# One weight pool for all stages, gate banks copied out beside the statistics, and pooled inputs ahead of their gates

## Chip, cores and metric

The kernel runs on one core of one Trainium2 chip. The metric is the device time of one execution in microseconds (us), as the median of several runs; lower is better. One further execution was recorded by the hardware profiler, and all rows below are of that one. Engines are named as the profile names them: PE is TensorE (PEld its weight loads), DVE VectorE, ACT ScalarE, POOL GpSimd, SP SyncE, which here issues every DMA.

## What is computed

One inference step of a single layer for 1024 prompt tokens and 8 x 4 decode tokens, 1056 rows in all, in float32:

```python
h = rmsnorm(x, norm_w)
pool_in, pool_z, qk_pre, v, o_pre, m_z, if_pre, gate_pre = jnp.split(h @ w_in, SPLIT_OFFSETS, axis=-1)
a, pool_hist_new = multiscale_pool(pool_in, pool_hist, pos0, pool_w, pool_scale)
a = (a * jax.nn.silu(pool_z)) @ w_pool_down
qk, conv_hist_new = causal_conv_silu(qk_pre, conv_hist, conv_w, conv_b)
...                                       # mLSTM over chunks of 128 tokens: gate statistics, then attention
bm = (hc * jax.nn.silu(m_z)) @ w_mlstm_down
g_a, g_b = jnp.split(jax.nn.sigmoid(gate_pre), 2, axis=-1)
x = x + (g_a * a + g_b * bm) @ w_out
x = x + (pe @ w_ple) * jax.nn.sigmoid(rmsnorm(x, ple_norm_w) @ w_ple_gate)
```

`multiscale_pool` takes causal means over windows of 2, 4, 8 and 16 tokens, one window for each of four groups of 256 channels, subtracts the input, and multiplies each group by a 256 x 256 matrix `pool_w`. The decode tokens also update a 512 x 512 state C for each of 8 sequences and 4 heads (32 states of 1 MB, each read and written once).

## The kernel before

Every large product is split: a weight tile of 4 x 128 rows and 256 columns comes by one 512 KB DMA into a buffer with the tag `wraw`, ACT rounds it to `whi` (line 370) and DVE forms the rest, `wlo` (line 376); PE then runs three matmuls for each product of hi and lo parts (`mm3`, lines 383 to 385). `load_w` (from line 396) does this for a block of 256 output columns, two such tiles for a depth of 1024; `fm` then runs two halves (f = 0, 1) of 128 output features, each over 1056 tokens in 3 pieces of 352 columns (72 matmuls) or 4 pieces of 264 (96 matmuls). Each piece fills a PSUM bank of the tag `mm`, of which there are two, and an eviction (`ev`) empties it; so PE may run one piece ahead of the evictions.

The stages that matter here, in the order of the program:

1. The first projections (lines 163 and 221), 28 blocks of seven steps, in pools `weights1` (seven `wraw`, three `whi`, three `wlo`) and `gemm`. Beside the last three steps `gate_rows` (line 757) projects the eight input and forget gates and stores them (lines 764, 766).
2. `weights1` is closed, `const2` and `weights2` (two `wraw`, three `whi`, three `wlo`) are opened where it lay, and `masks` (lines 504 to 527) forms a few constants on POOL and DVE.
3. `merge_gates` over six groups of 256 gate columns. Each half is evicted by three sigmoids on ACT (line 1311) into a tile `sz` of 1056 columns, of which there are two, and stored to `sgD` (line 1313). After each `fm` the function `tick` moves a background generator on. At first that is `gates`: the gates' statistics, a chain of small instructions on DVE, ACT, PE and SP, with Exp and Ln on ACT, and its end, 12 loads of `dt` (line 882), DVE sums on them (886, 888), four exponentials of 1536 columns (line 905) and their stores (907). Then the generator is the prompt's attention, and after it `sample`, the decode states.
4. `pool_branch`, for each of four groups: pool_z by `load_w` and `fm` with Silu into two `sz` (line 1219), pool_in by `load_w` and `fm` with the windowed sums on DVE (1260 to 1275) and the split into `poh` and `pol`, and the pooled product with `pool_w`, 36 matmuls on `poh` and `pol`, whose eviction (line 1286) multiplies `sz`; `sz` is then stored to `actD` (1289). Beside this run the 32 decode states: a load of `ct` (line 1166), PE lines 1168 and 1172, DVE line 1173, a store (1176).
5. The last two gate groups, the down projections and the tail, which the change does not touch.

The engine queues are filled in an order that a list scheduler fixes when the kernel is built: it takes, for each engine, the ready instruction that comes first in the program by its own model of time. Each engine then runs its queue strictly in that order, so an instruction that waits holds all behind it. SP's queue of DMA issues is such a queue too.

Of the kernel before, what the change touches and what calls it, by code (L numbers as in the profile page):

```python
# [12 lines left out]
AF = mybir.ActivationFunctionType  # L13
# [5 lines left out]
P = 128  # L19
# [101 lines left out]
class FeatBlock(Block):  # L121
# [10 lines left out]
    def prep(self, i):  # L132
# [11 lines left out]
        elif i in "db":  # L144
            x = tr.t(tr.wp, [P, 4, 256], "wraw", bufs=tr.nraw)
            tt(out=x[:, :, f1], in0=r1[:, :, f2], in1=r2[:, :, f2], op=ALU.add)
            tt(out=x[:, :, f2], in0=r1[:, :, f1], in1=x[:, :, f1], op=ALU.subtract)
            hi, lo = tr.split_w(x)
            self.w["d"], self.w["b"] = [(hi[:, :, f], lo[:, :, f]) for f in (f1, f2)]
            self.x = x  # L150
        elif i in ("c", "01"):
            tt(out=r1[:, :, f2], in0=r1[:, :, f1], in1=r1[:, :, f2], op=ALU.subtract)
            tt(out=r1[:, :, f1], in0=r2[:, :, f1], in1=self.x[:, :, f2], op=ALU.add)
            hi, lo = tr.split_w(r1)
            self.w["01"], self.w["c"] = [(hi[:, :, f], lo[:, :, f]) for f in (f1, f2)]
# [28 lines left out]
class TokBlock(Block):  # L184
# [15 lines left out]
    def prep(self, i):  # L200
        tr, r = self.tr, self.raw
        tt = tr.nc.vector.tensor_tensor
        if i == "d":
            self.x = tr.t(tr.wp, [P, 4, 256], "wraw", bufs=tr.nraw)
            tt(out=self.x, in0=r[0][1], in1=r[1][1], op=ALU.add)
# [135 lines left out]
class Trunk:  # L341
    def __init__(self, ctx, nc, tc, I, O):
        self.ctx, self.nc, self.tc, self.I, self.O = ctx, nc, tc, I, O
        self.n = 0
        self.bg = None
        self.held = None


# [6 lines left out]
    def t(self, pool, shape, tag, dt=F32, bufs=1):  # L355
        self.n += 1
        return pool.tile(list(shape), dt, name=f"{tag}_{self.n}", tag=tag, bufs=bufs)

    def mmps(self):
# [36 lines left out]
    def load_w(self, ap, n, scale=None):  # L396
# [4 lines left out]
        for k0 in range(0, kt, 4):  # L401
            kk = min(4, kt - k0)
            raw = self.t(self.wp, [P, 4, 256], "wraw", bufs=self.nraw)
            nc.sync.dma_start(raw[:, :kk, :n], ap[k0 * P:(k0 + kk) * P].rearrange("(k p) n -> p k n", p=P))
# [99 lines left out]
    def masks(self):  # L504
        nc, c = self.nc, self.cp2
        one = self.t(self.mk, [P, P], "one")
        nc.gpsimd.memset(one, 1.0)
        tri = self.t(self.mk, [P, P], "tri")
        nc.gpsimd.affine_select(out=tri, in_=one, pattern=[[1, P]], compare_op=ALU.is_ge, fill=0.0, base=0,
# [13 lines left out]

        cnt = self.t(self.mk, [P, 16], "cnt")
        nc.gpsimd.iota(cnt, pattern=[[1, 16]], base=1, channel_multiplier=0, allow_small_or_imprecise_dtypes=True)
# [3 lines left out]
    def norm_in(self, blocks):  # L529
# [103 lines left out]

        ab = self.t(self.wp, [P, 4, 256], "wraw", bufs=self.nraw).rearrange("p (i a) n -> p i (a n)", i=2)
        a = [ab[:, 0], ab[:, 1], st(), st()]
# [56 lines left out]
    def raw_w(self, w, c0, f, ks=(0, 1)):  # L692

        out = []
        for k in ks:
            r = self.t(self.wp, [P, 4, 256], "wraw", bufs=self.nraw)
            c = c0 + 256 * f
# [70 lines left out]
    def gates(self):  # L768
# [67 lines left out]
        mc = mcs[:, 0:1]  # L836
        yield True
        nc.vector.scalar_tensor_tensor(out=m[:, :L], in0=b[:, :L], scalar=mc, in1=m[:, :L], op0=ALU.add, op1=ALU.max)
        bm = self.t(a, [R, W], "gbm")
# [359 lines left out]
    def pool_branch(self):  # L1199
# [8 lines left out]
        for g in range(4):  # L1208
            win = 2 ** (g + 1)
            h1 = self.t(a, [DB * PH, 256], "ph1")  # L1210
            nc.sync.dma_start(h1, hist[:, g * 256:(g + 1) * 256])
            w = self.load_w(I["w_in"][:, O_PZ + g * 256:O_PZ + (g + 1) * 256], 256)
            sz = []
            for f in range(2):
                z = self.t(a, [P, NT], "sz", bufs=2)

                def ev(j, ps, z=z):
                    s = slice(j * CW, (j + 1) * CW)
                    nc.scalar.activation(z[:, s], ps[:, :CW], AF.Silu)
                self.fm(w, f, self.hmov, ev)  # L1220
                sz.append(z)
            w = self.load_w(I["w_in"][:, O_PIN + g * 256:O_PIN + (g + 1) * 256], 256)
            pooled = []
            for f in range(2):
# [6 lines left out]
                def ev(j, ps, f=f, ft=ft, ph=ph, pl=pl, prev=prev):  # L1231
# [46 lines left out]
                    self.lo(pl[:, c], po, ph[:, c])  # L1278
                self.fm(w, f, self.hmov, ev, CH)
            w = self.load_w(I["pool_w"][g], 256)  # L1280
            for f in range(2):
# [19 lines left out]
    def merge_gates(self, groups):  # L1301
        nc, I = self.nc, self.I
        for gg in groups:
            x, g = gg // 4, gg % 4
            w = self.load_w(I["w_in"][:, O_GA + gg * 256:O_GA + (gg + 1) * 256], 256)
            for f in range(2):
                z = self.t(self.pp, [P, NT], "sz", bufs=2)

                def ev(j, ps, z=z):
                    s = slice(j * CW, (j + 1) * CW)  # L1310
                    nc.scalar.activation(z[:, s], ps[:, :CW], AF.Sigmoid)  # L1311
                self.fm(w, f, self.hmov, ev)
                nc.sync.dma_start(self.sgD[x][g * 2 + f], z)

# [233 lines left out]
    def run(self):  # L1548
# [26 lines left out]
        self.xp, _x = self.pool("sums", "right")  # L1575
        self.wp, _w = self.pool("weights1")
        self.gp, _g = self.pool("gemm")
        self.nraw, self.nsb, self.nz = 7, 6, 7
        blocks = []
# [14 lines left out]
        _g.close()  # L1594
        _w.close()
        _x.close()
# [3 lines left out]
        self.hcS = self.t(self.cp2, [P, H, 4, NS], "hcS")  # L1600
        self.wp, _w = self.pool("weights2")
        self.nraw = 2
        self.mk, _m = self.pool("mask", "right")
        self.masks()
        _m.close()
        self.ap_, _a = self.pool("gates", "right")
# [4 lines left out]
        def rest():  # L1611
            self.rate = 1.6
            yield from gates
            _a.close()
            self.atp, _at = self.pool("attn", "right")
# [36 lines left out]
        self.tail_ple()  # L1652
        for st in (_l, _f, _w, _c2, _c, _ps):
            st.close()
# [24 lines left out]
```

## Time and profile before

| | |
|---|---|
| median of 3 runs | 2232.88 us (2228.46 to 2236.81) |
| the profiled execution | 2232.33 us |
| its span, first to last instruction | 2230.6 us |
| PE busy | 2159.6 us |
| DVE busy | 1257.2 us |
| ACT busy | 900.8 us |
| mean granted TensorE clock, as a share of full speed | 0.990 |

The span is the time that the instructions of the profile cover; 1.7 us of the execution lie outside it. Busy time of PE is modelled for pipelined matmuls, so a busy PE is not one at its peak, and a gap of PE is a lower bound of what was lost there: after a long gap the rows show matmuls at half the clock.

### The profile page before, as it was taken

The page shows a single profiled execution, that of the slowest core. Times are in us where ns is not written, and L with a number is a line of the kernel's source. Part 1 is how long each engine was busy: PE and PEld are TensorE (multiplying, and loading weights), DVE is VectorE, ACT ScalarE, POOL GpSimd, SP SyncE. Part 2 cuts the span into 40 slices and gives each one's busy share as a digit, 9 for nine tenths or more (in the row PEclk, how much of TensorE's full clock was granted, in tenths as well). Part 3 has the DMA queues.
Part 4 walks back from the last instruction along what each step waited for, and adds up shares of the span by engine and source line. Part 5 has one row for each costly group of instructions (what it writes and reads, how often), then busy time and mean ns, then how long its engine had stood idle before and what let it go on. Part 6 is the DMA issues. An engine that isn't in the chain of part 4 may idle for free.

```text
span 2230.6 us, 40176 instructions
## 1 busy us (share of the span) xinstructions
PE 2159.6 (97%) x16407; PEld 2054.8 (92%) x16407; DVE 1257.2 (56%) x2172; ACT 900.8 (40%) x1791; POOL 122.7 (6%) x335
## 2 busy tenths in 40 slices
PE   7999999999999999899999899999988999999998
PEld 6899999999999999899999798787778999999998
DVE  6855576456746565446566675576563243543645
ACT  5645455444635353633333343222223331213443
POOL 1100001000101000000000100000000000000000
PEclk9999999999999999999999999999999999999999
DMA  4233333333233331675655645887774343323112
GB/s 153 85 107 108 102 103 96 108 102 115 93 107 96 112 93 38 195 245 160 196 158 161 204 140 175 294 289 261 252 265 162 97 139 102 108 97 104 53 48 83
DMA packets 238601, 312.72 MB, mean 140 GB/s; under 512 B 13994, under 2 KB 170066, under 8 KB 238416
## 3 DMA queue, kind: packets, MB, share of 16 engines
q1 hardware_dynamic: 238416, 310.15, 42.8%
q8 instruction: 129, 2.11, 0.4%
q14 instruction: 56, 0.46, 0.1%
HBM read 200.01 MB, written 110.45 MB: 139 GB/s over the span
## 4 chain that ended last, share of the span: by engine, by line
PE 87%; DMA 6%; DVE 3%; ACT 2%; SPq 1%; issue 1%; POOL 0%; DVEq 0%; POOLq 0%; ACTq 0%
PE mm L221 21%; PE mm L163 14%; PE mm L383 12%; PE mm L385 12%; PE mm L384 12%; PE num L1168 2%; PE misc L953 2%; PE num L383 1%; PE kv L383 1%; PE num L384 1%; PE num L385 1%; PE kv L384 1%; PE kv L385 1%; PE kv L1172 1%; DMA o<-oD 1%; DMA ct<-state_mlstm_C 1%
## 5 line engine op out<-in xcount | busy, mean ns | idle before, releaser
L376 DVE TENSOR_TENSOR wlo<-wraw,whi 128x1024 fp32r<-128x1024 f32 (+1 forms) x220 | 238.7, 1086 | 228.7 <-ACT whi L370 222.9
L370 ACT ACTIVATE whi<-wraw 128x1024 fp32r<-128x1024 f32 (+1 forms) x220 | 209.2, 951 | 340.8 <-PE mm L221 107.1
L383 PE MATMUL mm<-hh,whi 128*128 128x352 f32 (+1 forms) x832 | 265.7, 319 | 14.5 <-ACT sz L1311 9.0
L385 PE MATMUL mm<-hh,wlo 128*128 128x352 f32 (+1 forms) x832 | 262.6, 316 | 0.0
L384 PE MATMUL mm<-hl,whi 128*128 128x352 f32 (+1 forms) x832 | 261.7, 315 | 0.0
L221 PE MATMUL mm<-wlo,hh 128*128 128x256 f32 x768 | 216.1, 281 | 0.0
L221 PE MATMUL mm<-whi,hl 128*128 128x256 f32 x768 | 215.9, 281 | 0.0
L221 PE MATMUL mm<-whi,hh 128*128 128x256 f32 x768 | 214.6, 279 | 0.0
L383 PEld LDWEIGHTS mm<-hh,whi 128*128 128x128 f32 x832 | 158.8, 191 | 28.5 <-ACT sz L1311 11.3
L384 PEld LDWEIGHTS mm<-hl,whi 128*128 128x128 f32 x832 | 159.2, 191 | 5.7 <-issue 4.4
L385 PEld LDWEIGHTS mm<-hh,wlo 128*128 128x128 f32 x832 | 158.7, 191 | 5.5 <-issue 4.2
L323 DVE SCALAR_TENSOR_TENSOR z<-z,vcols,z 128x556 f32<-128x556 f32 x192 | 146.8, 794 | 8.4 <-ACT z L321 6.6
L163 PE MATMUL mm<-hh,whi 128*128 128x264 f32 x512 | 148.4, 290 | 1.0 <-DVE z L179 0.6
L163 PE MATMUL mm<-hl,whi 128*128 128x264 f32 x512 | 146.2, 286 | 0.4 <-DVE hl L376 0.3
L163 PE MATMUL mm<-hh,wlo 128*128 128x264 f32 x512 | 145.5, 284 | 0.0
L221 PEld LDWEIGHTS mm<-whi,hh 128*128 128x128 f32 x768 | 144.7, 188 | 0.0
L221 PEld LDWEIGHTS mm<-whi,hl 128*128 128x128 f32 x768 | 144.6, 188 | 0.0
L221 PEld LDWEIGHTS mm<-wlo,hh 128*128 128x128 f32 x768 | 144.3, 188 | 0.2
L1173 DVE SCALAR_TENSOR_TENSOR ct<-ct,dec,kv 128x512 f32<-128x512 f32 x128 | 93.4, 744 | 70.9 <-PE kv L1172 61.3
L385 PE MATMUL mm<-mvhB,wlo 128*128 128x352 f32 x384 | 123.2, 322 | 0.0
L384 PE MATMUL mm<-mvlB,whi 128*128 128x352 f32 x384 | 123.0, 322 | 0.0
L383 PE MATMUL mm<-mvhB,whi 128*128 128x352 f32 x384 | 122.1, 324 | 0.0
(462 smaller groups left out, 6071.6 us busy)
## 6 DMA issues: line engine op xcount, KB each, us to landing
wraw<-w_in SPq DMA_DIRECT2D x112, 512.0 KB
ct<-state_mlstm_C SPq DMA_DIRECT2D x32, 1024.0 KB
new_C_sample<-ct SPq DMA_DIRECT2D x32, 1024.0 KB
qkD<-z SPq DMA_DIRECT2D x64, 256.0 KB
qk<-qkD SPq DMA_DIRECT2D x16, 1024.0 KB
sgD<-sz SPq DMA_DIRECT2D x16, 528.0 KB
sg<-sgD SPq DMA_DIRECT2D x16, 528.0 KB
vD<-z SPq DMA_DIRECT2D x32, 256.0 KB
```

The lines of the kernel that those rows point to most:

```text
L163: self.tr.nc.tensor.matmul(ps[:, j, :CH], lhsT=st[:, k], rhs=mv[k][:, c], start=start and k == 0 and n == 0, stop=stop and k == 3 and n == ...
L221: self.tr.nc.tensor.matmul(ps[:, t // 2, t % 2 * 256:t % 2 * 256 + 256], lhsT=st[k][:, c], rhs=mv[:, k], start=start and t % 2 == 0 and k ...
L323: nc.vector.scalar_tensor_tensor(out=acc, in0=z[:, o:o + tot], scalar=wc(o), in1=acc, op0=ALU.mult, op1=ALU.add)
L370: self.nc.scalar.activation(out, in_, AF.Copy)
L376: self.nc.vector.tensor_tensor(out=out, in0=in_, in1=hi.bitcast(F32), op=ALU.subtract)
L383: mm(ps, lhsT=sh, rhs=mh, start=start, stop=False)
L384: mm(ps, lhsT=sh, rhs=ml, start=False, stop=False)
L385: mm(ps, lhsT=sl, rhs=mh, start=False, stop=stop)
L953: nc.tensor.matmul(out, lhsT=qk[:, 4 + d, i * L:(i + 1) * L], rhs=qk[:, d, i * L:], start=d == 0, stop=d == 3)
L1168: nc.tensor.matmul(num[32 * d:32 * d + 32, 0, :], lhsT=qm[:, b * P + d * NS:b * P + (d + 1) * NS], rhs=ct[:, d, :], start=b == 0, stop=b = ...
L1172: nc.tensor.matmul(kv, lhsT=km[:, d * P:(d + 1) * P], rhs=vst, start=True, stop=True)
L1173: nc.vector.scalar_tensor_tensor(out=ct[:, d, :], in0=ct[:, d, :], scalar=self.dec[:, h * DB + b, 1:2], in1=kv, op0=ALU.mult, op1=ALU.add)
```

## The change

Three things are changed. (1) `weights1` and `weights2` become one pool `weights` that stays open to the end (two `wraw`, three `whi`, three `wlo`), and a pool `weights1` with five more raw buffers (`wrawx`) that closes after the first projections. `raw()` hands out the seven in turn, and the two alone afterwards. `masks` moves into the generator `gates`, behind its first pause, and takes its scratch tiles from the pool of that generator. (2) While the generator is inside `gates`, `merge_gates` evicts a bank by a plain copy on DVE, and one sigmoid on ACT over the whole tile of 1056 columns follows. The flag is read before each `fm`. (3) In `pool_branch` the block that forms pool_z moves from ahead of pool_in to behind it.

```diff
+    def raw(self):
+        self.nraw += 1
+        if self.wx is not None and self.nraw % 7 > 1:
+            return self.t(self.wx, [P, 4, 256], "wrawx", bufs=5)
+        return self.t(self.wp, [P, 4, 256], "wraw", bufs=2)
...
@@ load_w, raw_w, Block.prep, norm_in
-            raw = self.t(self.wp, [P, 4, 256], "wraw", bufs=self.nraw)
+            raw = self.raw()
...
@@ gates
         mc = mcs[:, 0:1]
         yield True
+        self.masks()
...
@@ pool_branch
-            w = self.load_w(I["w_in"][:, O_PZ + g * 256:O_PZ + (g + 1) * 256], 256)
-            sz = []
-            for f in range(2):
-                ...
             w = self.load_w(I["w_in"][:, O_PIN + g * 256:O_PIN + (g + 1) * 256], 256)
             pooled = []
             ...
                 self.fm(w, f, self.hmov, ev, CH)
+            w = self.load_w(I["w_in"][:, O_PZ + g * 256:O_PZ + (g + 1) * 256], 256)
+            sz = []
+            for f in range(2):
+                z = self.t(a, [P, NT], "sz", bufs=2)
+                ...
+                self.fm(w, f, self.hmov, ev)
+                sz.append(z)
             w = self.load_w(I["pool_w"][g], 256)
...
@@ merge_gates
-                def ev(j, ps, z=z):
+                plain = self.stats
+                def ev(j, ps, z=z, plain=plain):
                     s = slice(j * CW, (j + 1) * CW)
-                    nc.scalar.activation(z[:, s], ps[:, :CW], AF.Sigmoid)
+                    if plain:
+                        nc.vector.tensor_copy(z[:, s], ps[:, :CW])
+                    else:
+                        nc.scalar.activation(z[:, s], ps[:, :CW], AF.Sigmoid)
                 self.fm(w, f, self.hmov, ev)
+                if plain:
+                    nc.scalar.activation(z, z, AF.Sigmoid)
                 nc.sync.dma_start(self.sgD[x][g * 2 + f], z)
...
@@ run
-        self.wp, _w = self.pool("weights1")
+        self.wp, _w = self.pool("weights")
+        self.wx, _wx = self.pool("weights1")
...
-        _w.close()
+        _wx.close()
+        self.wx = None
...
-        self.wp, _w = self.pool("weights2")
-        self.nraw = 2
-        self.mk, _m = self.pool("mask", "right")
-        self.masks()
-        _m.close()
...
+            self.stats = True
             yield from gates
+            self.stats = False
```

## Rows read from the trace of the kernel before

**Rows 1.** The page: busy time, share of the span and instructions of each engine.

```profile
PE 2159.6 (97%) x16407; PEld 2054.8 (92%) x16407; DVE 1257.2 (56%) x2172; ACT 900.8 (40%) x1791; POOL 122.7 (6%) x335
```

**Rows 2.** Busy time by stretch (start:end, length, then each engine), granted clock, DMA.

```profile
895.00:899.40 4.40, 0.00 (x1) 0.01 (x1) 0.03 (x1) 2.12 (x3) 3.19 (x6) 0.82 0.99 315
899.40:909.60 10.20, 10.20 (x48) 9.88 (x48) 5.99 (x13) 7.06 (x8) 0.00 (x0) 0.74 0.42 123
909.60:933.90 24.30, 24.30 (x159) 23.67 (x158) 7.62 (x32) 10.69 (x18) 0.00 (x0) 1.00 0.51 140
933.90:950.20 16.30, 12.59 (x74) 11.44 (x72) 9.50 (x37) 16.09 (x17) 0.00 (x0) 1.00 0.96 300
...
1190.00:1345.00 155.00, 142.44 (x1062) 134.92 (x1061) 109.75 (x224) 63.26 (x131) 13.00 (x19) 0.97 0.53 167
```

**Rows 3.** What PE waited for from 895 to 1000: total us, times, longest.

```profile
PE mm L383 <- ACT whi L370: 4.5, 1, 4.5
PE mm L383 <- ACT sz L1311: 3.7, 4, 2.2
```

**Rows 4.** SP's queue in order of time: start, us, line, DMA, count.

```profile
893.41 1.02 SPq L404 DMA_DIRECT2D wraw<-w_in  x2
...
921.41 13.21 SPq L882 DMA_DIRECT2D dt<-bmD  x12
...
936.52 0.45 SPq L1313 DMA_DIRECT2D sgD<-sz  x1
...
945.49 0.33 SPq L1313 DMA_DIRECT2D sgD<-sz  x1
```

**Rows 5.** ACT in order of time, while PE waits for its evictions.

```profile
934.54 1.28 ACT L1311 ACT_TABLE_LOAD   x1
935.83 0.46 ACT L1311 ACTIVATE sz<-mm 128x352 f32<-128x352 f32 x1
936.32 1.28 ACT L905 ACT_TABLE_LOAD   x1
937.61 1.49 ACT L905 ACTIVATE dt<-dt 128x1536 f32<-128x1536 f32 x1
...
958.30 0.47 ACT L1311 ACTIVATE sz<-mm 128x352 f32<-128x352 f32 x1 [2.67 <-issue]
```

**Rows 6.** Groups of instructions by line and shape, 895 to 1400: busy us, mean ns.

```profile
L370 ACT ACTIVATE whi<-wraw 128x1024 fp32r<-128x1024 f32 x16 | 17.0, 1060 | 16.5 <-PE mm L384 13.2 <-DMA wraw<-w_in 3.2
L1025 DVE COPY C<-kv 128x256 f32<-128x256 f32 x16 | 6.7, 418 | 1.1 <-PE kv L385 1.1
L872 DVE COPY tok<-misc 128x128 f32<-128x128 f32 x1 | 0.3, 292 | 0.1
```

**Rows 7.** DVE in order of time: the first instructions of the masks.

```profile
890.08 0.79 DVE L517 TENSOR_REDUCE bcol<-ident 32x8 f32<-32x32 f32 x4
```

**Rows 8.** Stretches of the four pooled products, and the gate columns after the last.

```profile
1402.50:1416.00 13.50, 11.76 (x70) 8.12 (x69) 11.95 (x22) 3.51 (x9) 0.34 (x2) 1.00 1.03 367
1480.30:1492.50 12.20, 10.92 (x64) 8.21 (x61) 11.34 (x23) 2.90 (x8) 1.41 (x2) 1.00 0.77 261
1555.20:1568.00 12.80, 10.99 (x64) 8.25 (x61) 12.46 (x26) 2.69 (x7) 0.67 (x3) 1.00 0.81 277
1632.20:1654.10 21.90, 16.27 (x78) 9.92 (x75) 17.88 (x37) 5.28 (x12) 0.59 (x3) 0.84 0.77 257
1654.10:1688.50 34.40, 34.40 (x207) 31.68 (x206) 11.26 (x16) 10.49 (x18) 0.55 (x1) 1.00 0.77 265
```

**Rows 9.** PE in order of time: last pool_in matmul of the fourth group.

```profile
1630.97 0.28 PE L385 MATMUL mm<-hh,wlo 128*128 128x264 f32 x1
```

**Rows 10.** DVE in order of time: weights' and pooled input's low parts, fourth group.

```profile
1630.96 1.22 DVE L376 TENSOR_TENSOR wlo<-wraw,whi 128x1024 fp32r<-128x1024 f32 x1
1632.10 0.49 DVE L1260 TENSOR_TENSOR win<-win 128x324 f32<-128x324 f32 x1
1632.51 1.22 DVE L376 TENSOR_TENSOR wlo<-wraw,whi 128x1024 fp32r<-128x1024 f32 x1
...
1649.34 0.42 DVE L376 TENSOR_TENSOR pol<-po,poh 128x264 fp32r<-128x264 f32 x1
```

**Rows 11.** ACT in order of time: the split that feeds the first of those.

```profile
1629.48 1.06 ACT L370 ACTIVATE whi<-wraw 128x1024 fp32r<-128x1024 f32 x1 [0.45 <-PE mm L384]
```

**Rows 12.** What PE waited for from 1340 to 1760: total us, times, longest.

```profile
PE mm L383 <- ACT sz L1311: 6.9, 2, 5.3
PE num L1168 <- DMA ct<-state_mlstm_C: 6.0, 4, 3.7
```

More of the change, by code (lines that the diff above doesn't have):

```diff
@@ L144, in prep @@
         elif i in "db":
-            x = tr.t(tr.wp, [P, 4, 256], "wraw", bufs=tr.nraw)
+            x = tr.raw()
             tt(out=x[:, :, f1], in0=r1[:, :, f2], in1=r2[:, :, f2], op=ALU.add)
@@ L203, in prep @@
         if i == "d":
-            self.x = tr.t(tr.wp, [P, 4, 256], "wraw", bufs=tr.nraw)
+            self.x = tr.raw()
             tt(out=self.x, in0=r[0][1], in1=r[1][1], op=ALU.add)
@@ L505, in masks @@
         nc, c = self.nc, self.cp2
-        one = self.t(self.mk, [P, P], "one")
+        one = self.t(self.ap_, [P, P], "one")
         nc.gpsimd.memset(one, 1.0)
-        tri = self.t(self.mk, [P, P], "tri")
+        tri = self.t(self.ap_, [P, P], "tri")
         nc.gpsimd.affine_select(out=tri, in_=one, pattern=[[1, P]], compare_op=ALU.is_ge, fill=0.0, base=0,
@@ L522, in masks @@
         nc.vector.tensor_scalar(out=self.smask, in0=self.smask, scalar1=-1.0, scalar2=-NEG, op0=ALU.add, op1=ALU.mult)
-        cnt = self.t(self.mk, [P, 16], "cnt")
+        cnt = self.t(self.ap_, [P, 16], "cnt")
         nc.gpsimd.iota(cnt, pattern=[[1, 16]], base=1, channel_multiplier=0, allow_small_or_imprecise_dtypes=True)
@@ L632, in norm_in @@
         st = lambda: self.t(g, [P, HH], "s", bufs=self.nsb)[:, :HT]
-        ab = self.t(self.wp, [P, 4, 256], "wraw", bufs=self.nraw).rearrange("p (i a) n -> p i (a n)", i=2)
+        ab = self.raw().rearrange("p (i a) n -> p i (a n)", i=2)
         a = [ab[:, 0], ab[:, 1], st(), st()]
@@ L695, in raw_w @@
         for k in ks:
-            r = self.t(self.wp, [P, 4, 256], "wraw", bufs=self.nraw)
+            r = self.raw()
             c = c0 + 256 * f
@@ L1211, in pool_branch @@
             nc.sync.dma_start(h1, hist[:, g * 256:(g + 1) * 256])
-            w = self.load_w(I["w_in"][:, O_PZ + g * 256:O_PZ + (g + 1) * 256], 256)
-            sz = []
-            for f in range(2):
-                z = self.t(a, [P, NT], "sz", bufs=2)
-                def ev(j, ps, z=z):
[L1218 to L1221, printed above, removed]
             w = self.load_w(I["w_in"][:, O_PIN + g * 256:O_PIN + (g + 1) * 256], 256)
@@ L1279, in pool_branch, with ev @@
                 self.fm(w, f, self.hmov, ev, CH)
+            w = self.load_w(I["w_in"][:, O_PZ + g * 256:O_PZ + (g + 1) * 256], 256)
+            sz = []
+            for f in range(2):
+                z = self.t(a, [P, NT], "sz", bufs=2)
+                def ev(j, ps, z=z):
+                    s = slice(j * CW, (j + 1) * CW)
+                    nc.scalar.activation(z[:, s], ps[:, :CW], AF.Silu)
+                self.fm(w, f, self.hmov, ev)
+                sz.append(z)
             w = self.load_w(I["pool_w"][g], 256)
@@ L1307, in merge_gates @@
                 z = self.t(self.pp, [P, NT], "sz", bufs=2)
-                def ev(j, ps, z=z):
+                plain = self.stats
+                def ev(j, ps, z=z, plain=plain):
                     s = slice(j * CW, (j + 1) * CW)
-                    nc.scalar.activation(z[:, s], ps[:, :CW], AF.Sigmoid)
+                    if plain:
+                        nc.vector.tensor_copy(z[:, s], ps[:, :CW])
+                    else:
+                        nc.scalar.activation(z[:, s], ps[:, :CW], AF.Sigmoid)
                 self.fm(w, f, self.hmov, ev)
+                if plain:
+                    nc.scalar.activation(z, z, AF.Sigmoid)
                 nc.sync.dma_start(self.sgD[x][g * 2 + f], z)
@@ L1575, in run @@
         self.xp, _x = self.pool("sums", "right")
-        self.wp, _w = self.pool("weights1")
+        self.wp, _w = self.pool("weights")
+        self.wx, _wx = self.pool("weights1")
         self.gp, _g = self.pool("gemm")
-        self.nraw, self.nsb, self.nz = 7, 6, 7
+        self.nraw, self.nsb, self.nz = -1, 6, 7
         blocks = []
@@ L1612, in rest @@
             self.rate = 1.6
+            self.stats = True
             yield from gates
+            self.stats = False
             _a.close()
@@ L1652, in run @@
         self.tail_ple()
-        for st in (_l, _f, _w, _c2, _c, _ps):
+        for st in (_l, _f, _c2, _w, _c, _ps):
             st.close()
```

## Prediction

> **What bounds the kernel now.** I read the busy times first: PE is busy for 2159.6 us of a span of 2230.6, its weight loads lie beside that, and no other engine is busy for more than 57% [rows 1]. The change takes no matmul away, so all it can move is the 71 us in which PE stands still and what its clock loses after such gaps. Next I read PE's waits and the table of stretches where the change acts. At the seam between the first projections and the gate columns PE has a gap of 4.4 us [rows 2], nearly all of it one wait of 4.5 for a weight's high part [rows 3]. The 48 matmuls behind it take 10.2 us at a mean granted clock of 0.74, while 159 of the next stretch take 24.3 at full clock (some of those are tiny), 0.153 each [rows 2]. At that rate the 48 would take 7.3, so the slow clock costs another 2.9. From 933.9 to 950.2 PE is busy 12.6 of 16.3 us: 3.7 go in four waits for the sigmoid that empties a bank [rows 2, 3]. In the pool stage PE rarely shows as idle, so I compared matmuls per microsecond. In the four stretches of the pooled product it does 70, 64, 64 and 78 in 60.4 us; the gate columns after them run 207 in 34.4, 6.0 per us, at which the 276 would take 46.0 [rows 8]. That is 14.4 us lost, about half of it in the fourth group. Together the addressable loss is 4.5 + 2.9 + 3.7 + 14.4 = 25.5 us, 1.1%.
>
> **Part 1, one weight pool.** The two loads for the first gate columns are issued at 893.41 [rows 4], when the last projection step is nearly over. In the changed kernel their buffers are two of the seven that the last block no longer reads, so the loads (the same two of 512 KB on SP) can go out some steps earlier, and their split (1.06 on ACT [rows 6], 1.22 on DVE [rows 10], twice) lies beside projection matmuls. If that happens, the 4.5 and the 2.9 both go. What is late next: the PSUM banks for these columns come from a pool that opens when the projections' banks close, so the last of them have to be emptied, about 1 us by the ACT copy of 1024 columns [rows 6]; and the first half of group 0 is still emptied by sigmoids on ACT, which stand among the statistics' Exp and Ln, each change of function a load of 1.28 [rows 5], up to two of them in front of an eviction, less the one piece that PE may run ahead: 0 to 2.6. Bounds 0 to -7.4; I take -5. Moving the masks costs PE nothing: a few DVE instructions, four of them 0.79 together [rows 7], now stand beside the statistics, where DVE is busy 7.6 of 24.3 us [rows 2]; without that cover it would be under 3 us on a chain that PE does not wait for at that point.
>
> **Part 2, plain copies.** Four halves are now emptied by 12 DVE copies. No copy of 352 columns is in the trace; those of 256 and 128 take 0.418 and 0.292 [rows 6], so by the slope I estimate 0.51, against the sigmoid's 0.46 [rows 5]. That is less than the 3.7 us (24 matmuls at 0.153) which PE takes to fill the other bank, so the price itself is hidden. What goes is the order on ACT: there a sigmoid stands behind an exponential of 1.49 and two table loads of 1.28 [rows 5], 4.05 together, more than the 3.7 that PE gives it. That is the 3.7 us of waits, and all of it can go. What is added: one sigmoid of 1056 columns for each half, which I scale from 1024 columns at 1.06 [rows 6] to 1.1, with a load of 1.28 ahead of it, and only then the store. The two `sz` tiles make the next but one half wait for that store. On SP, 12 loads of `dt` occupy 13.2 us, and one gate store is issued right behind them, at 936.52; another went out at 945.49 [rows 4], and an eviction at 958.30 stood 2.67 us for nothing that the profile names [rows 5], which I read as the wait for that store's landing, 12.8 us after its issue. So a copy may wait too, now on DVE, with the `dt` sums queued behind it and the attention's first loads behind those. The store can go 2.4 us after the last copy; whether it gets ahead of the 12 loads is the scheduler's choice. If it does, nothing. If not, it lands up to 2.4 + 13.2 + 12.8 = 28.4 us after that copy; PE needs 11.0 for a half (72 at 0.153) and 7.3 for two pieces before it stands still, so it could stand for 10, 6 more than now. Bounds -3.7 to +6; I take -2, nearer to the first since the statistics move forward with their evictions.
>
> Beside this the ScalarE: Activation LUTs page of the Trainium skill (What ACT_TABLE_LOAD costs) counts a drain of about 1.38 us on top of the load, 2.66 for each change of set; here the sigmoid starts 0.01 us after the load's end [rows 5], so the trace does not agree, and by the page the four whole-tile sigmoids would each be ready 1.4 later, which would make this part -0.6 where I have -2.
>
> **Part 3, pool_z behind pool_in.** Nothing is added; two loads on SP, two splits, 144 matmuls and six Silu evictions for each group go behind pool_in's. Now the pooled product follows pool_in at once, and its input comes late: in the fourth group the last matmul of pool_in starts at 1630.97 [rows 9] and the last low part of the pooled input at 1649.34 [rows 10], 18.4 us later. With pool_z between them PE has 144 matmuls at 0.153, 22 us, to do first, so that latency is covered even there. What is late next: (a) the second half of pool_z's weights reuses the buffers of pool_in's first half. Its split would stand where one stands now: high part from 1629.48 [rows 11], low part 1630.96 to 1632.18 [rows 10], 1.2 us behind the last pool_in matmul; the 12 matmuls on the first half last 1.8, so it is just in time. (b) The decode states: PE waited 6.0 us in four waits for `ct` loads in this stage [rows 12], which the new order does not shorten. (c) The eviction of the pooled product itself. I leave 4.4 of the 14.4 for these and take -10. Bounds: -14.4, and -3 if the state loads hold PE wherever it runs ahead.
>
> **The rest.** The gate columns are what PE has to do beside attention, and they run out: from 1190 to 1345 PE is busy 142.4 of 155 us, 8% idle [rows 2]. Seven microseconds saved ahead of that lengthen it by as much: +0.6. The 6.9 us that PE waits at the last gate groups [rows 12] stay; as the order of all queues is drawn anew I allow 3 either way.
>
> **Sum.** -5 - 2 - 10 + 0.6 = -16.4 against 2232.3 of the profiled execution, 2215.9; the median of the runs, 2232.9, lies 0.55 above it, so 2216. Best bounds from that median: -7.4 - 3.7 - 14.4 - 3 + 0.6 gives 2205; worst: 0 + 6 - 3 + 0.6 + 3 gives 2239.5.
>
> **Rivals.**
> - *The pool stage is held by the decode states.* Each state is a load, matmuls, a DVE pass and a store in three buffers; if these set the pace, pool_z only moves the wait. For it: the `ct` waits, and a DMA share of 0.77 to 1.03 in the pooled stretches [rows 8]. Against it: right after the last of them PE runs 34.4 us without a gap at a share of 0.77 [rows 8]. Part 3 falls to -3: 2232.9 - 9.4 = 2223.5, within 0.5%.
> - *The gate store stands behind the `dt` loads.* Part 2 becomes +6 instead of -2: 2232.9 - 8.4 = 2224.5, within 0.5%. For it the order of now [rows 4]; against it that the evictions ahead come earlier.
> - *Slower: pool_z's weights queue behind the windowed sums on DVE.* If the low part of the second half comes behind the whole chain of pool_in instead of among it, PE waits in every group for what it waits for now, but with 12 matmuls for cover instead of a pooled product that it can start by pieces: 18.4 - 1.8 = 16.6 in the fourth group, and some 8 in each of the others, in proportion to their stretches of 12 to 13 us against 21.9 [rows 8]: 41 us against the 14.4 saved, with the other parts 2232.9 - 7 + 0.6 + 26.6 = 2253. It decides once DVE's backlog at the end of pool_in exceeds 1.8 us ahead of that split. Against it: in the fourth group, the fullest, two weight splits get through within 1.5 us between window sums [rows 10].
> - *The first loads stay late.* If something else of the seam holds the gate columns (banks, the statistics on SP), part 1 is 0: 2232.9 - 11.4 = 2221.5, at the edge of 0.5%.
>
> **How the numbers follow.** I take 0.5% (11 us, below about 2221.7 or above 2244) as what a measurement of this kernel can tell from no change. Forecast, with the mixtures around it down to the last rival: 0.62 for times below 2221.7. The first two rivals 0.13 and 0.10, the late first loads 0.07 (half of it on either side of the line), the slower one 0.08. So faster 0.65, same 0.27, slower 0.08. The range takes in the best bound and leaves the slower rival and the worst bound out: 2205 to 2234.
>
> **What would show it.** Right: no wait of PE for a weight's high part at the seam and a granted clock of 1.00 behind it; no load of ACT tables between two evictions there, DVE copies near 0.51; the gap from 934 to 950 gone; the pooled stretches at 6 matmuls per us, about 6 to 9 us each, with the last low part of the pooled input long before them. Wrong: PE waiting on DVE copies of `sz` with a gate store late on SP; a wait for `wlo` at the start of pool_z; longer waits for `ct`. The sum is wrong if the busy time of PE shrinks its gaps as said and the span does not follow, that is if the gaps come back at the last gate groups.

## The result, and the profile after

The changed kernel takes 2217.8 us in the median of 6 runs (2215.1 to 2223.2), beside 2231.7 for the kernel before, now also in the median of 6: a ratio of 0.9939, with a 95% interval of 0.9920 to 0.9958. A second series, on the chip of pool_only and move_only below, gave 0.9952 (0.9935 to 0.9969). The forecast of 2216 and its range hold. But the parts did not come out as they were priced, and that is what the rest is about.

The profiled execution took 2219.3 us, its span 2217.6. The busy times on the page of after:

```profile
PE 2152.3 (97%) x16407; PEld 2057.3 (93%) x16407; DVE 1265.4 (57%) x2184; ACT 893.4 (40%) x1780; POOL 127.3 (6%) x335
```

No matmul is gone, as against [rows 1]. The stretches by busy time, after: the seam, the gate columns beside the statistics, the four pooled products, and the last two gate groups.

```profile
896.49:909.60 13.11, 13.11 (x86) 12.82 (x85) 4.83 (x21) 10.09 (x13) 0.00 (x0) 1.00 0.49 145
909.60:928.80 19.20, 19.20 (x124) 18.48 (x122) 7.01 (x19) 7.82 (x13) 0.00 (x0) 1.00 0.41 118
928.80:932.20 3.40, 0.13 (x2) 0.06 (x1) 3.40 (x14) 1.48 (x1) 0.00 (x0) 1.00 1.05 306
932.20:950.20 18.00, 18.00 (x102) 17.81 (x103) 10.89 (x38) 10.04 (x9) 0.00 (x0) 0.91 0.87 281
1405.20:1414.10 8.90, 8.90 (x57) 7.45 (x56) 8.15 (x13) 2.85 (x4) 0.00 (x0) 1.00 0.82 275
1477.20:1487.70 10.50, 9.17 (x60) 7.65 (x57) 7.05 (x12) 1.60 (x4) 0.00 (x0) 1.00 0.99 349
1549.50:1558.70 9.20, 9.20 (x59) 7.82 (x58) 8.61 (x15) 2.29 (x5) 0.00 (x0) 1.00 0.85 282
1626.20:1635.10 8.90, 8.90 (x58) 7.47 (x55) 7.43 (x12) 2.40 (x5) 0.00 (x0) 1.00 1.03 380
1635.10:1697.90 62.80, 55.78 (x325) 50.91 (x325) 22.74 (x39) 19.09 (x35) 0.55 (x1) 0.97 0.62 211
```

The loads for the first gate columns and the loads of `dt` on SP's queue, after (start, us, line, DMA, count):

```profile
857.23 4.51 SPq L412 DMA_DIRECT2D wraw<-w_in  x2
...
918.89 9.74 SPq L891 DMA_DIRECT2D dt<-bmD  x9
928.73 0.88 SPq L1329 DMA_DIRECT2D sgD<-sz  x1
929.65 2.32 SPq L891 DMA_DIRECT2D dt<-bmD  x3
```

The gap at the seam and the slow clock behind it [rows 2] are gone: PE is busy for all of the first two stretches at full clock. A hole of 3.4 us is new at 928.8, and the clock is 0.91 in the stretch behind it. The pooled products take 8.9, 10.5, 9.2 and 8.9 us where they took 13.5, 12.2, 12.8 and 21.9 [rows 8], at 5.7 to 6.5 matmuls per us.

PE's waits after, from 895 to 1000 (first line) and from 1340 to 1745 (the others): total us, times, longest.

```profile
PE mm L391 <- DVE sz L1323: 3.3, 1, 3.3
...
PE mm L391 <- ACT sz L1325: 7.0, 2, 4.4
PE num L1177 <- DMA ct<-state_mlstm_C: 5.9, 6, 1.7
PE mm L391 <- ACT bm L1388: 3.0, 1, 3.0
PE mm L391 <- ACT u L1239: 1.5, 1, 1.5
```

The wait for a weight's high part and the four for sigmoids [rows 3] have become one wait for a plain copy. The waits for decode states and at the last gate groups add up to what they were [rows 12]. No wait for a weight's low part is in the list.

To see where the 13 us of the span went, I cut each execution at three places that every kernel has: the last matmul of the first projections, the first matmul of the decode states (which reads `qs` and `ks`), and the last matmul on `poh`. In the kernel after these rows of PE are:

```profile
896.37 0.28 PE L221 MATMUL mm<-whi,n4l 128*128 128x256 f32 x1
...
1340.82 0.90 PE L1098 MATMUL misc<-qs,ks 128*32 128x32 f32 x32 [0.64 <-ACT t2k L1074]
...
1634.91 0.32 PE L393 MATMUL mm<-poh,wlo 128*128 128x352 f32 x1
```

In the kernel before they are these:

```profile
894.66 0.28 PE L221 MATMUL mm<-whi,n4l 128*128 128x256 f32 x1
...
1345.84 0.90 PE L1089 MATMUL misc<-qs,ks 128*32 128x32 f32 x32 [0.64 <-ACT t2k L1065]
...
1653.50 0.32 PE L385 MATMUL mm<-poh,wlo 128*128 128x352 f32 x1
```

The head (end of the first row to start of the second) fell from 450.9 to 444.2 us, the pool stage (to the end of the third) from 308.0 to 294.4, and the rest (to the end of the span) rose from 576.8 to 582.4: -6.7, -13.6, +5.6. The projections themselves ended 1.7 later; over all executions below that place varies from 894.8 to 897.4 with no regard to the kernel. -6.7 - 13.6 + 5.6 + 1.7 = -13.0. The pool stage and the rest by busy time, in the kernel before and then after, show that 16 matmuls moved from the one to the other:

```profile
1345.84:1653.82 307.98, 296.49 (x1933) 239.47 (x1934) 192.19 (x398) 89.13 (x177) 14.77 (x55) 0.98 0.73 255
1653.82:2230.60 576.78, 558.97 (x3999) 545.52 (x3997) 249.27 (x499) 185.00 (x439) 16.62 (x27) 0.99 0.32 107
```

```profile
1340.82:1635.23 294.41, 285.32 (x1917) 240.46 (x1918) 188.48 (x390) 87.13 (x175) 14.43 (x56) 0.99 0.76 258
1635.23:2217.60 582.37, 562.86 (x4015) 547.40 (x4013) 255.24 (x508) 186.93 (x441) 16.66 (x27) 0.99 0.33 110
```

### The profile page after: what moved, and what is told of

It is laid out like the page before. It is cut to its first block, busy times and chain, and to the rows that moved or that the text cites. A ratio compares the mean times of both kernels' runs of the same rounds, so it can differ in the third digit from the quotient of the medians.

```text
span 2217.6 us, 40176 instructions
## 1 busy us (share of the span) xinstructions
PE 2152.3 (97%) x16407; PEld 2057.3 (93%) x16407; DVE 1265.4 (57%) x2184; ACT 893.4 (40%) x1780; POOL 127.3 (6%) x335
## 4 chain that ended last, share of the span: by engine, by line
PE 86%; DMA 8%; DVE 3%; ACT 1%; issue 1%; SPq 0%; POOL 0%; DVEq 0%; POOLq 0%; ACTq 0%
PE mm L221 22%; PE mm L163 15%; PE mm L391 12%; PE mm L393 12%; PE mm L392 12%; DMA ct<-state_mlstm_C 2%; DMA new_C_sample<-ct 2%; PE misc L962 1%; PE num L1177 1%; PE num L391 1%; DMA o<-oD 1%; PE num L392 1%; PE num L393 1%; PE kv L391 1%; PE kv L392 1%; PE kv L393 1%
## 5 line engine op out<-in xcount | busy, mean ns | idle before, releaser
L384 DVE TENSOR_TENSOR wlo<-wrawx,whi 128x1024 fp32r<-128x1024 f32 (+1 forms) x116 | 124.0, 1069 | 129.2 <-ACT whi L378 128.7
L378 ACT ACTIVATE whi<-wrawx 128x1024 fp32r<-128x1024 f32 (+1 forms) x116 | 108.7, 937 | 176.3 <-PE mm L163 71.4
L378 ACT ACTIVATE whi<-wraw 128x1024 fp32r<-128x1024 f32 (+1 forms) x104 | 100.3, 964 | 182.3 <-PE mm L392 95.5
L384 DVE TENSOR_TENSOR wlo<-wraw,whi 128x1024 fp32r<-128x1024 f32 (+1 forms) x104 | 114.8, 1103 | 89.2 <-ACT whi L378 81.6
```

The lines of the kernel that those rows point to most:

```text
L378: self.nc.scalar.activation(out, in_, AF.Copy)
L384: self.nc.vector.tensor_tensor(out=out, in0=in_, in1=hi.bitcast(F32), op=ALU.subtract)
```

## Experiments

All medians and ratios in one table; the last three columns are the three stretches of the profiled execution, found as above. Beside the first two rows the runs were made in three series (undo_pool, undo_copies, undo_move and hc_in_place; pool_only, move_only, act_copy and changed_again; the other in_place kernels), in which the kernel before took 2234.2, 2232.7 and 2231.6 us, so kernels of different series are compared by their ratios. A ratio is formed from all runs of its series and is not the quotient of the two medians: for pool_only that would be 0.9990.

| kernel | median us | ratio to before (95%) | head | pool stage | rest |
|---|---|---|---|---|---|
| before | 2231.7 | 1 | 450.9 | 308.0 | 576.8 |
| after | 2217.8 | 0.9939 (0.9920 to 0.9958) | 444.2 | 294.4 | 582.4 |
| changed_again | 2220.9 | 0.9952 (0.9935 to 0.9969) | 443.7 | 291.3 | 581.5 |
| undo_pool | 2218.4 | 0.9933 (0.9920 to 0.9946) | 447.3 | 292.4 | 582.5 |
| undo_copies | 2220.8 | 0.9941 (0.9929 to 0.9953) | 446.9 | 294.5 | 582.4 |
| undo_move | 2229.8 | 0.9983 (0.9974 to 0.9991) | 442.9 | 314.0 | 575.0 |
| pool_only | 2230.4 | 0.9996 (0.9983 to 1.0010) | 441.9 | 311.7 | 577.3 |
| move_only | 2221.9 | 0.9959 (0.9945 to 0.9973) | 450.6 | 292.3 | 579.6 |
| act_copy | 2221.0 | 0.9955 (0.9939 to 0.9972) | 441.5 | 297.8 | 584.0 |
| hc_in_place | 2207.1 | 0.9882 (0.9870 to 0.9895) | 446.2 | 291.5 | 572.7 |
| in_place_again | 2204.9 | 0.9879 (0.9862 to 0.9897) | 443.6 | 292.3 | 572.3 |
| in_place_before | 2221.9 | 0.9952 (0.9934 to 0.9969) | 450.3 | 308.3 | 564.3 |
| in_place_undo_pool | 2207.1 | 0.9890 (0.9874 to 0.9906) | 447.4 | 291.3 | 569.5 |
| in_place_dt8 | 2203.2 | 0.9868 (0.9848 to 0.9887) | 441.5 | 292.8 | 568.8 |

One part is undone in undo_pool, undo_copies and undo_move, and one is made alone in pool_only and move_only.

**undo_pool**: two pools again, masks at the seam.

```diff
-        self.wp, _w = self.pool("weights")
-        self.wx, _wx = self.pool("weights1")
+        self.wp, _w = self.pool("weights1")
+        self.wx = None
...
+        self.wp, _w = self.pool("weights2")
+        self.mk, _m = self.pool("mask", "right")
+        self.masks()
```

> The changed kernel with its first part undone: two weight pools again, the second opened at the seam, and the masks formed there. Theory: the seam's gap comes back whole, a wait for a weight's high part of about 4.5 us at the first gate columns and the slow clock behind it, another 2.9, so 2217.8 + 7.4 = 2225. Rival A (the prediction's own number): 5 us, 2222.8. Rival B: the last gate groups wait for the decode states' end and give back what is gained ahead of them, so the seam is worth 2 to 3 us at the end: 2220.

The wait for the weights came back whole, and yet the kernel is as fast as with the one pool. Part of the reason is in PE's waits from 880 to 1000 in this kernel: the copies now cost 0.8 instead of 3.3.

```profile
PE mm L391 <- ACT whi L378: 4.5, 1, 4.5
...
PE mm L391 <- DVE sz L1322: 0.8, 1, 0.8
```

In the head the pool is worth 3.1 us beside the copies (447.3 against 444.2), not 7.4. At the end nothing is left of it that the medians could tell. All three numbers that were expected (2220 to 2225) were too high; the lowest, rival B's 2220, is a ratio of 0.9947 and just outside the interval.

**undo_copies**: sigmoids empty every bank.

```diff
-                plain = self.stats
+                plain = False
```

> The changed kernel with its second part undone: a sigmoid on ACT empties each gate bank everywhere. Theory: the 3.7 us of waits for sigmoids come back and the one wait of 3.3 us for a copy goes, so 2217.8 + 0.4 = 2218.2, no measurable change. Rival A (the prediction's number for this part): 2 us, 2219.8. Rival B: the wait for a copy is only the order of this schedule, and the sigmoids among the statistics cost all they cost before: 2221.5.

No measurable difference: 0.9941 against 0.9939 and 0.9952. PE has one wait of 5.0 for a sigmoid in place of the one of 3.3 for a copy, at the same place. Theory held in time; that the sigmoids would wait as four small ones did not.

**undo_move**: pool_z ahead of pool_in.

```diff
+            w = self.load_w(I["w_in"][:, O_PZ + g * 256:O_PZ + (g + 1) * 256], 256)
...
+                self.fm(w, f, self.hmov, ev)
+                sz.append(z)
             w = self.load_w(I["w_in"][:, O_PIN + g * 256:O_PIN + (g + 1) * 256], 256)
...
-            w = self.load_w(I["w_in"][:, O_PZ + g * 256:O_PZ + (g + 1) * 256], 256)
...
-                sz.append(z)
```

> The changed kernel with its third part undone: pool_z ahead of pool_in. Theory: the pooled stretches lose again what they lost before, 14 us over the four groups, and the last gate groups and the first down product, which now wait about 5 us more than they need, give 4 to 5 of it back: 2217.8 + 9.5 = 2227. Rival A: the extra waits at the last gate groups have another cause and stay, 2217.8 + 14 = 2232. Rival B: the move by itself is worth only the 3 us of a stage that the decode states hold: 2221.

The ratio 0.9983 lies 0.0031 to 0.0044 above the changed kernel's two, 7 to 10 us: near the theory's 9.5, short of rival A's 14 and above rival B's 3. The pool stage lost 20 us (314.0 against 294.4), and the rest gave 7 back (575.0 against 582.4).

**pool_only** and **move_only**: the first and the third part, each alone, by the same edits.

> The kernel before with the first part alone. If the parts add up, the seam's 7.4 us are saved: a ratio of 0.9967 to the kernel before. Theory, after the undone first part left the changed kernel almost as fast: the gate columns only reach the statistics 7 us earlier and wait there instead (one wait of about 5 us for a sigmoid, where the kernel before has 3.7 in four), and a part of the rest is lost again beside attention; 2 to 4 us remain, a ratio of 0.9982 to 0.9991.

> The kernel before with the third part alone. Theory: the pool stage gains some 18 us by the end of its fourth product, and the last gate groups and the first down product give 6 to 7 of it back (decode matmuls that now fall there, and the loads through two raw buffers), so 11 us remain, a ratio of 0.9951. The prediction's 10 gives 0.9955. Rival: part of what undoing the move costs belongs to the other two parts, which bring the stage's start forward; then the move alone is worth 7 or less, 0.9969.

> The changed kernel itself once more, so that the others can be set beside it on the same chip. Every theory expects 2218 and a ratio of 0.994 to the kernel before, within 0.0015.

The changed kernel came again as expected, at 0.9952. The move alone gives 0.9959, 9.2 us of 2232.7 (6.0 to 12.3), which is near the theory and the prediction but leaves the rival's 0.9969 inside the interval. The pool alone is worth 0.9 us with an interval from -2.2 to 3.8, which rules out the 7.4 and reaches into the theory's 2 to 4, though its gap is gone from the trace and its profiled execution, one of its shortest at 2227.5 us, has a head of 441.9. What stands in PE's way in that head is on ACT, here in order of time (start, us, what, and in brackets the idle time before):

```profile
919.58 0.45 ACT L1325 ACTIVATE sz<-mm 128x352 f32<-128x352 f32 x1
926.23 1.28 ACT L914 ACT_TABLE_LOAD   x1 [6.20 <-DMA dt<-bmD]
928.00 1.48 ACT L914 ACTIVATE dt<-dt 128x1536 f32<-128x1536 f32 x1 [0.49 <-DVE dt L897]
929.50 1.28 ACT L1325 ACT_TABLE_LOAD   x1
930.80 0.82 ACT L1325 ACTIVATE sz<-mm 128x352 f32<-128x352 f32 x2
```

ACT stands idle for 6.2 us in front of an exponential whose data a `dt` load has still to bring, and two sigmoids that could have emptied two banks stand behind it; PE waits 4.3 us for them.

**act_copy**: the plain copies on ACT.

```diff
-                        nc.vector.tensor_copy(z[:, s], ps[:, :CW])
+                        nc.scalar.activation(z[:, s], ps[:, :CW], AF.Copy)
```

> The changed kernel with the plain copies on ACT instead of DVE; the whole-tile sigmoids stay. Theory: the wait of 3.3 us is the order of DVE's queue, where a copy stands behind the sums on the statistics' loads; on ACT a copy stands behind at most one exponential of 1.49 us and needs no table load, so PE has no wait for a gate bank: 2217.8 - 3 = 2215. Rival: the copy waits for the store of the tile's last contents, and does so on any engine: 2218, with a wait of about 3 us for ACT.

Neither held: PE waits 3.4 us, 2.7 of them at once, and the time is that of the changed kernel. These are the rival's numbers, but not its cause. The copies stand on ACT behind the same exponential:

```profile
928.45 1.28 ACT L914 ACT_TABLE_LOAD   x1 [3.56 <-DMA dt<-bmD]
930.24 1.48 ACT L914 ACTIVATE dt<-dt 128x1536 f32<-128x1536 f32 x1 [0.50 <-DVE dt L897]
931.62 0.80 ACT L1323 ACTIVATE sz<-mm 128x352 f32<-128x352 f32 x2
```

**in_place_dt8** (beside in_place_again): two loads of `dt` for each head instead of three; the third one's sums read the second's data.

```diff
-            for x in range(3):
+            for x in (0, 2):
                 nc.sync.dma_start(dt[:, :, x], rows[min(x, 1)].partition_broadcast(P))
...
+                nc.vector.tensor_scalar(out=dt[:, j, 1], in0=dt[:, j, 2], scalar1=col(3, 2 * j), scalar2=None,
+                                        op0=ALU.add)
                 for x in (0, 2):
...
-                nc.vector.tensor_scalar(out=dt[:, j, 1], in0=dt[:, j, 1], scalar1=col(3, 2 * j), scalar2=None,
-                                        op0=ALU.add)
```

> The in-place kernel with 8 instead of 12 loads for the statistics: the third of them that repeats the second is left out and its sums read the second's copy; everything is still computed. Theory: PE's one wait of 3.3 to 4.1 us for a gate bank is a wait for these loads, which a sum, or an exponential, ahead of the copy stands waiting for; with a third of them gone they arrive 3 us sooner and the wait falls to 1 us or none: 2207 - 3 = 2204, ratio 0.987. Rival: the wait is the order of the queue behind the sums themselves, whose number has not changed: wait and time as in the in-place kernel.

> The changed kernel with the attention's outputs loaded in place, once more, as the base for the other three on the same chip. Every theory expects 2207 and a ratio of 0.988 to the kernel before, within 0.0015.

The wait stayed at 3.3 (3.7 in in_place_again): the rival held on this point. DVE in order of time in in_place_dt8 shows why:

```profile
926.87 0.29 DVE L894 TENSOR_SCALAR dt<-dt,tok 128x128 f32<-128x128 f32 x1 [3.33 <-DMA dt<-bmD]
...
932.01 0.34 DVE L897 SCALAR_TENSOR_TENSOR dt<-dt,tok,cmask 128x128 f32<-128x128 f32 x1
932.27 0.51 DVE L1323 COPY sz<-mm 128x352 f32<-128x352 f32 x1
```

The first data come no earlier than with twelve loads (924.64 in in_place_again), and from 926.87 on DVE works through sums, with 0.4 us of idle time, until the copy has its turn at 932.27. So the copy pays for its place in the queue: first for the first load, then for the sums put ahead of it. (A kernel with the copy ahead of the sums was not run.) The time, 0.9868 against 0.9879, can't be told apart.

**hc_in_place**: one edit more on the changed kernel. Each output of attention that the down projection reads was loaded into one of two raw buffers (for the first four, the two `sz` tiles of the last gate groups), and is now loaded into the buffer of its low part and split there.

```diff
-            raw = self.t(pool, [P, NT], tag, bufs=2)
-            self.nc.sync.dma_start(self.halves(raw), self.hcD[k // 4][:, k % 4, :].rearrange("p (a n) -> p a n", a=2))
-            out.append(self.split(raw, slot, T))
+            mp = self.mpA if slot == "A" else self.mpB
+            hi = self.t(mp, [P, NT], "mvh" + slot, F32R, bufs=4)
+            lo = self.t(mp, [P, NT], "mvl" + slot, F32R, bufs=4)
+            raw = self.halves(lo.bitcast(F32))
+            self.nc.sync.dma_start(raw, self.hcD[k // 4][:, k % 4, :].rearrange("p (a n) -> p a n", a=2))
+            self.hi(self.halves(hi), raw)
+            self.lo(self.halves(lo), raw, self.halves(hi))
+            out.append((hi, lo))
```

> The changed kernel with one more edit: the attention's outputs for the down projection are loaded straight into the buffer of their low part and split there, so that no load waits for one of two raw buffers. Theory: the chain of loads through two buffers holds ACT's queue at the last gate groups and at the first down product; without it the waits of 4.4 and 3.0 us go and part of the 2.6: 2217.8 - 7 = 2211. Rival: ACT's queue is held there by the decode outputs, which are ready at 1676 whatever the loads do, and PE waits as before: 2217 to 2219.

2207.1 and, in the second series, 2204.9: more than expected. SP's queue shows the four loads at once (in the changed kernel they go out at 1657.49, 1665.65 and, two of them, 1673.88):

```profile
1643.63 2.97 SPq L1354 DMA_DIRECT2D mvlA<-hcD  x4
```

Of PE's waits from 1640 on, the 4.4 and the 3.0 are gone and 2.7 and 0.7 remain. The rest of the program fell from 582 to 572.5 us. This kernel is faster than both; with the eight `dt` loads it is 2203.2.

**in_place_before**: the same edit on the kernel before.

> The kernel before with the in-place loads alone. Theory: there too PE waited at the last gate groups and the first down product (5.3, 1.6 and 2.2 us), but less of the end depends on it: the stretch from the fourth pooled product to the end took 576.8 us before and 582.4 in the changed kernel, 572.6 with the in-place loads; some 2.3 of that difference are decode matmuls that fall there only in the changed kernel. So about 576.8 + 2 - 575 to 576.8 - 570.3 = 4 to 6.5 us are to be had, a ratio of 0.997 to 0.998. Rival: the chain costs the same in both, 10 us, 0.9955, and the change gave nothing back there.

The rival is nearest: 0.9952, 10.7 us, where the changed kernel gets 13 to 16 (0.9879 against 0.9952 and 0.9939), with intervals that overlap. The rest falls from 576.8 to 564.3. So the loads through two buffers cost both kernels about the same, and they are not why the change gives 5 us back at the end: with the loads in place the rest is still 4 to 8 us longer (568.8 to 572.7 against 564.3). I had to drop that theory. The stretch from the last pooled product to the first down matmul, in in_place_before and then in in_place_dt8, which has no wait of PE in it:

```profile
1655.90:1707.97 52.07, 50.49 (x309) 47.43 (x307) 17.93 (x33) 19.25 (x39) 0.55 (x1) 1.00 0.57 204
```

```profile
1631.60:1685.83 54.23, 54.23 (x328) 49.89 (x326) 23.29 (x41) 19.62 (x36) 0.55 (x1) 1.00 0.73 250
```

PE stands still for 52.07 - 50.49 = 1.6 us in the first and not at all in the second, where it does 19 matmuls more and works 54.23 - 50.49 = 3.7 us longer. 18 of the 19 are decode states. The groups of PE in the same two stretches:

```profile
L1172 PE MATMUL kv<-vst,km 96*128 96x512 f32 x4 | 1.4, 395 | 0.0
L1168 PE MATMUL num<-ct,qm 128*32 128x512 f32 x8 | 1.1, 605 | 0.0
```

```profile
L1181 PE MATMUL kv<-vst,km 96*128 96x512 f32 x14 | 5.3, 404 | 0.0
L1177 PE MATMUL num<-ct,qm 128*32 128x512 f32 x16 | 2.1, 605 | 0.0
```

In the kernel before they are 4 and 8 in this stretch, and in the changed kernel 12 and 16.

**in_place_undo_pool**: hc_in_place without the one pool.

> The in-place kernel with the one weight pool undone. It tells where the seam's 7.4 us go, which the medians of the other runs do not show at the end. Theory A, they are lost early: the gate columns that start 7 us sooner wait 3 to 4 us longer for what stands behind the statistics' loads, and the slow clock behind that wait and attention take most of the rest; then undoing costs 1 to 3 us here as well: a ratio of 0.989. Theory B, the chain of loads at the last gate groups swallowed them; without that chain undoing costs 5 to 7: 0.991.

0.9890 against 0.9879, 2.2 us between the medians: near theory A, and no sign that the late loads hid 5 to 7 us, though the two intervals overlap. Of the 7.4, the head has 447.4 - 443.6 = 3.8 left against in_place_again and 1.2 against hc_in_place, so most of it is lost within the head.

## Why the prediction was right, and where its steps were wrong

**The seam (part 1).** The mechanism came as forecast: the loads go out at 857.23, 36 us ahead of [rows 4], and the gate columns follow the last projection without a gap. The whole 7.4 was saved there (86 matmuls in the 13.11 us up to 909.6, where the kernel before does 48 in 14.6 [rows 2]); the rival that the first loads stay late is refuted. The price was wrong, -5 where undoing the part costs nothing that can be told from zero (2.2 us with the loads in place, and the part alone gives 0.9 with bounds of -2.2 and 3.8). The step that failed is its list of what is late next: it had PSUM banks and table loads, 0 to 2.6 us, and left out that columns which come 7 us sooner meet the `dt` loads before their data are there. Under the sigmoids the four waits, 3.7 [rows 3], became one of 4.3 (pool_only) and 5.0 (undo_copies), and under the copies 0.8 became 3.3, with slow clock behind it: 0.09 of 18 us, 1.6 by estimate. For the changed kernel that is 7.4 - 2.5 - 1.6 = 3.3, beside the 3.1 between the heads.

**The copies (part 2).** Their price was right: 0.52 each where 0.51 was estimated, the whole sigmoid 1.08 to 1.09 where it was 1.1, no table load between two of these evictions. (ACT loads the table at 921.57 for 1.28 us and the whole-tile sigmoid starts at 922.87, 0.02 after the load's end. The ScalarE: Activation LUTs page of the Trainium skill, What ACT_TABLE_LOAD costs, adds about 1.38 us for a drain; this trace does not show it either.) So was the hazard named, but not its mechanism: the text had a copy that waits for a store late on SP, with sums behind it. The store of the second half did go out among the `dt` loads, at 928.73 behind nine of them, and no wait follows from it. What came is the reverse: a copy that is ready stands behind sums. DVE in order of time, after:

```profile
922.73 0.17 DVE L883 TENSOR_SCALAR tok<-tok 128x32 f32<-128x32 f32 x1
925.45 0.35 DVE L895 SCALAR_TENSOR_TENSOR dt<-dt,tok,cmask 128x128 f32<-128x128 f32 x1 [2.54 <-DMA dt<-bmD]
927.24 0.35 DVE L895 SCALAR_TENSOR_TENSOR dt<-dt,tok,cmask 128x128 f32<-128x128 f32 x1 [1.44 <-DMA dt<-bmD]
...
930.79 0.87 DVE L895 SCALAR_TENSOR_TENSOR dt<-dt,tok,cmask 128x128 f32<-128x128 f32 x3
931.58 0.51 DVE L1323 COPY sz<-mm 128x352 f32<-128x352 f32 x1
```

What the part brings beside the pool is nothing that can be told, where -2 was taken: undone it gives 0.9941, the changed kernel 0.9939 and 0.9952.

In these executions the two parts do not add up. Beside neither the head is 450.3 to 450.9 (three executions); with the copies alone 447.3 and 447.4; with the pool alone 441.9 and 446.9; with both 442.9 to 446.2 (five). Each takes 3 to 6 us off, both take 6.5 off, and the forecast's 7 for the two, less the 0.6 beside attention, is that: by luck, as neither the -5 nor the -2 is what its part is worth. At the end less is left: the changed kernel lies 0.0007 to 0.0020 below move_only, 1.5 to 4.5 us. Where the remainder is lost behind the head is not settled. With pool_z first the pool stage took 312 and 314 us behind a short head and 308 behind a long one, as if the decode states set its end; with pool_in first it takes 291 to 295 behind either (298 in act_copy, where one wait of 2.8 for DVE's `kw` is new).

**pool_z behind pool_in (part 3).** The number was right, -10 against 9.2 alone and 7 to 10 undone. The reason for leaving 4.4 of the 14.4 was not. Residue (a), weights just in time, did not come: no wait for a low part, so the slower rival is refuted, and with it that DVE's backlog decides. Residue (b) is as said in this execution, 5.9 us of waits for decode states where there were 6.0 [rows 12]; in changed_again, the same program, they are 2.8, so it varies. But the stage gained more than 14.4: 293 us in the mean of ten executions with the move where it took 308, some 15. What takes it back lies behind the stage: the rest is 582.1 in the mean of six executions with the move and the old loads, and 576.4 in three without the move, 5.7 more, of which, by the view of stage and rest for each, PE is busy for 4.1 and idle for 1.6. The 16 decode matmuls that fall behind the stage only after the move are 3.1 of that, an estimate by the 3.7 us for 19. In the kernel before they ran within the pool stage: of the 78 matmuls in its last pooled stretch [rows 8] 34 are decode states, after it is 18 of 58. The prediction's 14.4 is net of that work, as it allows all 276 matmuls their time at 6.0 per us, so the 3.1 leave one stage, come back in the next and cancel. Without them the stage gained 12 of the 14.4, and 2.6 were lost behind it, where the prediction had nothing: it let the waits at the last gate groups stay and allowed 3 either way. So the 4.4 that it left out has about the right size, 2.4 + 2.6, but half of that arose where the prediction did not look for it; that the two agree is in part luck. Work that fills a stall moves when the stall goes. What causes the 2.6 is not settled.

**The rivals.** The decode states do not hold the new order: the pooled products run at full clock with one wait for `ct` among them, in the second. The gate store behind the `dt` loads, +6 for part 2, did not come: part 2 is near 0, between that and the forecast, and by another path.

**The sum.** -16.4 was forecast, -14.0 measured, and -10.7 in the second series. In the trace it is -6.7 - 13.6 + 5.6 + 1.7. Part 3 came (9.2 alone against 10), and the head fell as forecast. The step that failed is the one from there to the end: the prediction took a microsecond saved ahead of attention for one saved at the end, less 8% (the +0.6), while beside the move parts 1 and 2 are worth 1.5 to 4.5 us at the end, not 6.4. The intervals of these ratios do not quite exclude 6.4; those of pool_only do exclude the 5 of part 1 alone. With the 0.8 of part 3 this is about what the forecast was too low by, 2.4 us in the one series and 5.7 in the other.

## What to carry to other kernels

An operation that is moved forward in time is not faster by that alone: look up which loads the engines that serve it are waiting for at the new time, and whether an eviction stands in their queues behind an instruction that waits for one. Then it is the place in the queue that costs, on whichever engine it is put. When a stage gets shorter, count the work in it before and after: what ran in its stalls may now run behind it, and then a part of the stage's gain is not one of the program. And look along the whole list of PE's waits before choosing: one edit at the chain of loads behind the pool stage, untouched by this change, brought 11 to 16 us in either kernel.

## What the hardware showed that was not expected

Executions differ by where the granted clock falls. From 1180 to 1290 us, beside attention, the kernel before and then pool_only, whose code for this stage is the same:

```profile
1180.00:1290.00 110.00, 99.16 (x715) 93.67 (x714) 73.72 (x152) 43.39 (x91) 8.78 (x11) 0.95 0.56 175
```

```profile
1180.00:1290.00 110.00, 99.19 (x739) 92.65 (x738) 74.88 (x153) 45.93 (x95) 8.23 (x10) 1.00 0.62 191
```

PE is busy for the same time in both and gets 24 more matmuls done in the second. At 0.153 us each [rows 2] that is 3.7 us, and 0.95 over 110 us is 5.5 at most: as much as the parts of this change. One and the same program does it too, hc_in_place and then in_place_again, whose heads are 446.2 and 443.6:

```profile
1180.00:1290.00 110.00, 97.76 (x703) 91.08 (x703) 73.85 (x149) 44.86 (x92) 8.23 (x10) 0.95 0.57 178
```

```profile
1180.00:1290.00 110.00, 97.72 (x720) 91.15 (x719) 74.36 (x152) 45.39 (x93) 8.24 (x10) 0.97 0.60 183
```

The short head of pool_only's profiled execution is partly this (the clock over its head is 1.00, in the kernel before 0.98), and the two profiled executions of the changed kernel, 2217.6 and 2213.7 us of span, differ by 3.9 with the same program. So a single trace shows which wait goes, but not whether 5 us remain at the end; the medians do.
